# A two-layer hybrid decoder trunk: some accumulating DMAs become VectorE adds, and the FFN's four-pair groups, weight slots and raw tiles are dealt out anew

## The chip, the cores and the metric

The kernel runs on one core of a Trainium2 chip. The core's engines run side by side and wait for each other through semaphores: TensorE (PE, with the weight load PEld shown apart), VectorE (DVE), ScalarE (ACT), GpSimd (POOL) and SyncE (SP, which here only issues DMAs). The metric is device time in microseconds for one execution; lower is better.

## The reference

A residual stream of 256 tokens by 2048 goes through two layers, each a mixer and a SwiGLU FFN. All values are float32.

```python
def reference(x, ...):
    h = x
    for layer in range(DEPTH):              # DEPTH = 2
        xn = rms_norm(h, norm_mix[layer])
        if layer % 2 == 0:
            mix = swa_mlstm_mixer(xn, ...)  # sliding-window attention + mLSTM, out projection
        else:
            mix = forgetting_attention_mixer(xn, ...)
        h = h + mix
        h = h + swiglu(rms_norm(h, norm_ffn[layer]), w_gate[layer], w_up[layer], w_down[layer])
    return rms_norm(h, norm_final)

def swiglu(xn, w_gate, w_up, w_down):       # 2048 -> 5632 -> 2048
    return (jax.nn.silu(xn @ w_gate) * (xn @ w_up)) @ w_down
```

The change lies in the FFN.

## The kernel before, in words

**Products in split precision.** Each float32 matrix is used as a sum of two float32r parts, `hi` (a rounded copy, made by ScalarE) and `lo` (the rest, made by VectorE as `raw - hi`). A product is three matmuls: hi by hi, lo by hi, hi by lo (`three`, L531 to L534). The activations stand in `xh`, `xl` (and `mh`, `ml` for the FFN's hidden values), already split. The weights are streamed: `load_raw` (L134) issues a DMA from SP that brings 256 rows by 512 columns into a raw tile of 128 partitions by 2 by 512 (512 KB), `split_chunk` (L187, L188) or `split_plain` (L356, L357) splits it into a weight slot, a `hi` and a `lo` tile of the same size.

**Buffers.** In the FFN there are `RAWS` = 5 raw tiles. Weight slots are dealt out in a circle from `stock`: six of the pool `wp` and two (`more`) of the FFN's own pool, eight in all. A slot can be written again when TensorE has finished with it, and a raw tile can be loaded again when its readers have finished.

**Groups.** The hidden width 5632 is cut into 11 groups `g` of 512 columns. For a group, `pair_group` multiplies the activations (16 chunks of 128 rows, taken as 8 pairs) by `w_gate` and `w_up` at once. `PARTS` = (0, 3, 7, 11) cuts the groups into three parts: groups 0 to 2, 3 to 6, 7 to 10. Behind each part's groups stands its share of the down product, again by `pair_group`, over two column halves `n0`, and the result is added into `h`. In the last layer's last part the second half goes through `gemm` instead.

**Plain chunks and pairs.** An entry `(0, p)` of the order is plain: two chunks (gate and up) with 24 matmuls of 512 columns. An entry `(1, p)` is a *pair* in the sense used below: a scheme with seven products in place of eight, so 21 matmuls, for which sums of the weights and of the activations (`sums_of`) are needed. With `ra` the gate tile and `rb` the up tile, the weight side is:

```python
nc.gpsimd.dma_start(rb[:, 0, :], w[part, c0 : c0 + NB], accum_op=ALU.add)   # rb0 += ra0, from HBM
hg, lg = split_chunk(ra, NB)
split_plain(hu, lu, rb)
rb1 = rb0 - rb1             # L605, the third sum, written over rb
ra  = ra - rb1 (both halves)  # L607
split_plain(hc, lc, rb1); split_plain(hd, ld, ra)
```

The first sum is made by an *accumulating DMA* from GpSimd's queue (L599): it fetches the 256 KB of the gate weights a second time and adds them to what lies in `rb`. A pair takes four slots (`hg`, `hu`, `hc`, `hd`), a plain entry two. `ORDER` has three pairs in eight entries, `HEAVY` four; the groups in `DENSE` = (1, 4, 5, 8, 9) use `HEAVY`. `DOWN` gives the down product two pairs of six entries in the first part and three of eight in the others. So a layer has 38 pairs in the groups, and with 16 (layer 0) and 13 (layer 1) in the down products there are 105.

**Combining.** At a group's end ScalarE and VectorE join the products (`combine`, L555 to L559), add the plain sums (L671), apply SiLU (L673) and the product (L675); the hidden values are transposed by DMA and split into `mh`, `ml` by a `join` that is put off into the next group.

**What stands ahead of the FFN.** `out_proj` is the mixer's output projection; its results are added to `h` (L370), squared for the norm, turned by DMA transposes (L317), and split by `split_scaled` (L361, L362). Part of that is put off into the FFN's first group.

**Order.** The code is written in the order above; a scheduler then sets the order of each engine's instructions by its own estimates, so a change of one place can move instructions over a whole layer. Each engine runs its list strictly in order.

Of the kernel before, what the change touches and what calls it, by code (L numbers as in the profile page):

```python
# [17 lines left out]
P = 128  # L18
# [5 lines left out]
NB = 512  # L24
CK = 2
# [10 lines left out]
ORDER = ((0, 0), (1, 1), (0, 2), (1, 3), (0, 4), (1, 5), (0, 6), (0, 7))  # L36
HEAVY = ((1, 1), (0, 0), (1, 3), (0, 2), (1, 5), (0, 4), (1, 7), (0, 6))
FOURTH = 7
DENSE = (1, 4, 5, 8, 9)
DOWN = {  # L40
    6: ((0, 0), (1, 1), (0, 2), (1, 3), (0, 4), (0, 5)),
    8: ((0, 0), (1, 1), (0, 2), (1, 3), (0, 4), (1, 5), (0, 6), (0, 7)),
# [9 lines left out]
W_RAWS = 4  # L52
LATER = (6, 10, 3, 5)
LATER_DOWN = (5, 6)
RAWS = 5
P_JOIN = 4
COLD = 9
TURNED = (0,)
# [17 lines left out]
def trunk(  # L76
# [459 lines left out]
    def bank(par, name):  # L536
        return pm.tile([P, NB], F32, tag="pm", name=name) if par else pa.tile([P, NB], F32, tag="acc", name=name)

    def pair_group(fp, par, lhs, sums, mats, order, todo=(), halves=None, inner=None, raws=None):
        plain = [[bank(par, "acc") for _ in range(NT)] for _ in range(2)]  # L540
        begun = set()

        def fresh(*at):
            known = at in begun
            begun.add(at)
            return not known

        todo = list(todo)
        prods = None
        kinds = [kind for kind, _ in order]  # L550
        t0, t1 = slice(0, P), slice(P, 2 * P)

        def combine(prods):
            c = fp.tile([P, 4, NB], F32, tag="c", name="c", bufs=1)
            nc.scalar.copy(c[:, 0, :], prods[0])  # L555
            if halves is None:
                nc.vector.tensor_tensor(out=c[:, 1, :], in0=prods[3], in1=c[:, 0, :], op=ALU.add)
                nc.vector.tensor_tensor(out=c[:, 2, :], in0=prods[2], in1=c[:, 1, :], op=ALU.add)
                nc.vector.tensor_tensor(  # L559
                    out=c[:, 1:4:2, :],  # L560
                    in0=prods[1].rearrange("p (a n) -> p a n", a=1).broadcast_to([P, 2, NB]),
                    in1=c[:, 1:3, :],
                    op=ALU.subtract,
                )
                return c
            nc.vector.tensor_tensor(out=c[:, 2, :], in0=prods[3], in1=c[:, 0, :], op=ALU.add)
            nc.vector.tensor_tensor(out=c[:, 1, :], in0=prods[2], in1=c[:, 2, :], op=ALU.add)
            nc.vector.tensor_tensor(out=c[:, 3, :], in0=prods[1], in1=c[:, 1, :], op=ALU.subtract)
            nc.vector.tensor_tensor(out=c[:, 2, :], in0=prods[1], in1=c[:, 2, :], op=ALU.subtract)
            return c  # L570

        for pos, (kind, pair) in enumerate(order):
            k0 = 2 * pair
            if inner is not None and pos == len(order) - 1:
                c = combine(prods)
                inner()
            if not kind:
                last = pos == len(order) - 1
                walk = [(i, t) for i in range(CK) for t in range(NT)]
                if last:  # L580
                    walk.sort(key=lambda it: it[1])
                for m, (w, c0) in enumerate(mats):
                    hi, lo = load_chunk(w, k0, c0, NB)
                    run_due(todo, pos)
                    for i, t in walk:
                        ah, al = lhs(k0 + i)
                        ts = slice(t * P, (t + 1) * P)
                        three(
                            plain[m][t], ah[:, ts], al[:, ts], hi[:, i, :], lo[:, i, :],
                            fresh(m, t), last and i == CK - 1,  # L590
                        )
                continue
            first, last = 1 not in kinds[:pos], 1 not in kinds[pos + 1 :]
            if first:
                prods = [bank(1 - par, "prod") for _ in range(4)]
            ra, rb = (load_raw(w, k0, c0, NB, fp, W_RAWS if halves else RAWS, raws) for w, c0 in mats)
            if halves is None:
                (w, c0), part = mats[0], slice(k0 * P, (k0 + 1) * P)
                nc.gpsimd.dma_start(rb[:, 0, :], w[part, c0 : c0 + NB], accum_op=ALU.add)  # L599
            hg, lg = split_chunk(ra, NB)  # L600
            run_due(todo, pos)
            hu, lu = slot()
            if halves is None:
                split_plain(hu, lu, rb)
                nc.vector.tensor_tensor(out=rb[:, 1, :], in0=rb[:, 0, :], in1=rb[:, 1, :], op=ALU.subtract)  # L605
                both = rb[:, 1, :].rearrange("p (a n) -> p a n", a=1).broadcast_to([P, CK, NB])
                nc.vector.tensor_tensor(out=ra, in0=ra, in1=both, op=ALU.subtract)  # L607
                hc, lc = (a[:, 0, :] for a in slot())
                split_plain(hc, lc, rb[:, 1, :])
                hd, ld = slot()  # L610
                split_plain(hd, ld, ra)
                ht = [hu[:, 0, :], hd[:, 0, :], hc, hd[:, 1, :]]
                lt = [lu[:, 0, :], ld[:, 0, :], lc, ld[:, 1, :]]
            else:
                split_plain(hu[:, 1, :], lu[:, 1, :], rb[:, 1, :])
                nc.vector.tensor_tensor(out=ra[:, 0, :], in0=rb[:, 0, :], in1=ra[:, 0, :], op=ALU.add)
                nc.vector.tensor_tensor(out=rb[:, 0, :], in0=rb[:, 1, :], in1=rb[:, 0, :], op=ALU.subtract)
                nc.vector.tensor_tensor(out=rb[:, 1, :], in0=ra[:, 0, :], in1=rb[:, 1, :], op=ALU.subtract)
                nc.vector.tensor_tensor(out=ra[:, 1, :], in0=ra[:, 1, :], in1=rb[:, 1, :], op=ALU.subtract)
# [12 lines left out]
            three(prods[0], xa[:, t0], la[:, t0], hg[:, 0, :], lg[:, 0, :], first, last)  # L632
            three(plain[0][0], xb[:, t0], lb[:, t0], hg[:, 1, :], lg[:, 1, :], fresh(0, 0), False)
            three(plain[1][0], sh[3], sl[3], hu[:, 1, :], lu[:, 1, :], fresh(1, 0), False)
            three(prods[1], sh[0], sl[0], ht[0], lt[0], first, last)
            three(prods[2], sh[2], sl[2], ht[1], lt[1], first, last)
            three(prods[3], sh[1], sl[1], ht[2], lt[2], first, last)
            three(plain[0][1], xb[:, t1], lb[:, t1], ht[3], lt[3], fresh(0, 1), False)
        if inner is None:
            c = combine(prods)  # L640
        return plain, c

    def ffn(layer, fp, sx, x4, sd, key, todo, idx_next=None, key_next=None, finish=None):
# [8 lines left out]
        for g0, g1 in zip(PARTS, PARTS[1:]):  # L652
# [3 lines left out]
            for g in range(g0, g1):  # L656
# [6 lines left out]
                    [(w_gate[layer], g * NB), (w_up[layer], g * NB)],  # L663
                    HEAVY if g in DENSE else ORDER,
                    todo,
                )
                todo = []
                for m in range(2):
# [79 lines left out]
            for n0 in (0, 2):  # L748
                if end and idx_next is None and n0 == 2:
                    for n in (2, 3):  # L750
                        acc = new_acc()
                        gemm(acc, m_of, wd, n * NB, NB, 0, nk, nk, skew=3 if n == 3 else 1, halved=n == 3)
                        close(acc, n)
                    continue
                plain, c = pair_group(
                    fp, 1 - n0 // 2, m_of, sums_d, [(wd, n0 * NB), (wd, (n0 + 1) * NB)], order, todo
                )
                todo = []
                if end and idx_next is None:
                    gf = fp.tile([P, D], F32, tag="c", name="gf", bufs=1)  # L760
                    nc.gpsimd.dma_start(gf, norm_final.partition_broadcast(P))
                for t in range(NT):
                    o = h[:, t, n0 * NB : (n0 + 2) * NB]
                    nc.vector.tensor_tensor(
                        out=o, in0=c[:, 2 * t : 2 * t + 2, :].rearrange("p a n -> p (a n)"), in1=o, op=ALU.add
                    )
                for m in range(2):
                    close(plain[m], n0 + m)

    def close_layer(layer, w_out, idx, key, **rest):  # L770
        with tc.tile_pool(name=f"fp{layer}", bufs=2) as fp:
# [3 lines left out]
            x4 = fp.tile([P, 2, P], F32R, name="x4", bufs=1)  # L775
            todo = out_proj(w_out, idx, key, (*sx, x4, fp))
            sd = [fp.tile([P, nd, 4, P], F32R, tag=f"sd{i}", name=f"sd{i}", bufs=1) for i in range(2)]
            more = [[fp.tile([P, CK, NB], F32R, name=f"{a}{i}", bufs=1) for a in ("hi", "lo")] for i in range(2)]
            stock.extend(more + [slot() for _ in range(6)])
            ffn(layer, fp, sx, x4, sd, key, todo, **rest)  # L780
            stock.clear()
# [601 lines left out]
```

## Time and profile before

| | |
|---|---|
| median of three runs | 2097.1 us (2096.4 to 2097.92) |
| the profiled execution | 2095.33 us, of which 2093.6 us are its span |
| granted TensorE clock, mean | 0.998 |
| PE busy | 2072.1 us (99%) |
| DVE busy | 1794.4 us (86%) |
| ACT busy | 1384.1 us (66%) |
| accumulating DMAs (L599) | 76 of gate, 29 of down weights |
| HBM read | 436.21 MB |

Stretches are given as from:to in us from the start of the span. In a row of the profile, L599 is line 599 of the kernel's file, `out<-in` are the names of the tiles, `xN` the count of instructions, and `[5.27 <-DMA raw...]` the idle time of the engine just before and what ended it. Layer 0's FFN follows its `out_proj` near 330; its first part ends near 530, the second near 775 and the third near 1015. Layer 1's FFN begins near 1400, and its parts end near 1597, 1840 and 2045.

### The profile page before, as it was taken

The numbers are of one execution on the slowest core, as the hardware profiler recorded it, in microseconds if no ns is written. First come the engines' busy times: TensorE is split into PE (matmuls) and PEld (weight loads), VectorE is DVE, ScalarE is ACT, GpSimd is POOL, SyncE is SP. The second block draws the span as 40 slices with busy tenths as digits, with TensorE's granted clock in tenths as the row PEclk, the third lists the DMA queues.
The fourth block names the chain that finished last, engine by engine and source line by source line (L and its number), as shares of the span: only waits on it lengthen the run. The fifth ranks groups of instructions, "written<-read, shape, count | busy, mean of one in ns | idle before, by whom it ended". The sixth has DMA issues, their size and how long they took to land.

```text
span 2093.6 us, 27094 instructions
## 1 busy us (share of the span) xinstructions
PE 2072.1 (99%) x9443; PEld 1709.8 (82%) x9443; DVE 1794.4 (86%) x2217; ACT 1384.1 (66%) x1764; POOL 133.7 (6%) x171
## 2 busy tenths in 40 slices
PE   9999999999999999999999999999999999999998
PEld 8878887778888888888888888887788888888887
DVE  6788768988999998998899678578899999999995
ACT  6767677665567656667676776686655667557763
POOL 1010000000000000000000001000000000000000
PEclk9999999999999999999999999999999999999999
DMA  8666578777788777887676777597778777867864
GB/s 294 177 201 201 195 257 226 217 215 218 220 229 265 227 244 220 237 238 202 204 225 198 227 201 186 162 263 202 243 220 244 228 223 234 265 201 209 263 208 150
DMA packets 324698, 462.43 MB, mean 221 GB/s; under 512 B 108092, under 2 KB 116304, under 8 KB 324432
## 3 DMA queue, kind: packets, MB, share of 16 engines
q1 hardware_dynamic: 307088, 426.27, 64.8%
q0 software_dynamic: 16752, 33.33, 9.0%
q8 instruction: 74, 1.21, 0.2%
q10 hardware_dynamic: 720, 1.09, 0.1%
q14 instruction: 64, 0.52, 0.1%
HBM read 436.21 MB, written 2.12 MB: 209 GB/s over the span
## 4 chain that ended last, share of the span: by engine, by line
PE 75%; DVE 8%; DMA 6%; ACT 5%; issue 4%; SPq 0%; ACTq 0%; POOLq 0%; POOL 0%; DVEq 0%
PE acc L533 16%; PE acc L532 16%; PE acc L534 16%; PE prod L533 4%; PE prod L532 4%; PE prod L534 4%; PE acc L222 4%; PE acc L223 4%; PE acc L224 4%; DVE lo L188 2%; DVE lo L357 2%; DMA raw<-in_w_down_dram 2%; ACT hi L187 2%; DMA raw<-in_w_gate_dram 1%; ACT hi L356 1%
## 5 line engine op out<-in xcount | busy, mean ns | idle before, releaser
L188 DVE TENSOR_TENSOR lo<-raw,hi 128x1024 fp32r<-128x1024 f32 (+2 forms) x646 | 761.7, 1194 | 153.8 <-ACT hi L187 151.2
L187 ACT CAST hi<-raw 128x1024 fp32r<-128x1024 f32 (+2 forms) x646 | 651.6, 1026 | 319.8 <-PE acc L534 83.7
L533 PE MATMUL acc<-lo,xh 128*128 128x512 f32 x1260 | 491.7, 391 | 1.0 <-DVE lo L188 1.0
L534 PE MATMUL acc<-hi,xl 128*128 128x512 f32 x1260 | 490.1, 390 | 0.0
L532 PE MATMUL acc<-hi,xh 128*128 128x512 f32 x1260 | 478.6, 392 | 5.5 <-ACT hi L187 3.9
L356 ACT CAST hi<-raw 128x1024 fp32r<-128x1024 f32 (+1 forms) x329 | 291.4, 894 | 226.5 <-DVE raw L605 84.6
L357 DVE TENSOR_TENSOR lo<-raw,hi 128x1024 fp32r<-128x1024 f32 (+1 forms) x329 | 334.9, 1029 | 52.2 <-ACT hi L356 50.8
L532 PEld LDWEIGHTS acc<-hi,xh 128*128 128x128 f32 x1260 | 236.8, 188 | 58.8 <-ACT hi L187 7.7
L533 PEld LDWEIGHTS acc<-lo,xh 128*128 128x128 f32 x1260 | 236.8, 188 | 53.0 <-DVE lo L188 3.9
L534 PEld LDWEIGHTS acc<-hi,xl 128*128 128x128 f32 x1260 | 236.9, 188 | 48.9
L533 PE MATMUL acc<-lo,mh 128*128 128x512 f32 x466 | 181.6, 390 | 0.0
L534 PE MATMUL acc<-hi,ml 128*128 128x512 f32 x466 | 181.4, 389 | 0.0
L532 PE MATMUL acc<-hi,mh 128*128 128x512 f32 x466 | 175.8, 390 | 0.5 <-ACT hi L187 0.5
L607 DVE TENSOR_TENSOR raw<-raw 128x1024 f32<-128x1024 f32 x105 | 128.3, 1222 | 1.0
L599 POOL DMA_DIRECT2D raw<-in_w_gate_dram x76 | 65.1, 856 | 963.9 <-DMA raw<-in_w_up_dram 391.4
L223 PE MATMUL acc<-lo,mh 128*128 128x512 f32 (+1 forms) x322 | 126.3, 392 | 0.0
L222 PE MATMUL acc<-hi,mh 128*128 128x512 f32 (+1 forms) x322 | 125.8, 391 | 0.0
L224 PE MATMUL acc<-hi,ml 128*128 128x512 f32 (+1 forms) x322 | 123.7, 391 | 0.0
L532 PEld LDWEIGHTS acc<-hi,mh 128*128 128x128 f32 x466 | 87.5, 188 | 19.4 <-ACT hi L187 1.3
L533 PEld LDWEIGHTS acc<-lo,mh 128*128 128x128 f32 x466 | 87.5, 188 | 18.1
L534 PEld LDWEIGHTS acc<-hi,ml 128*128 128x128 f32 x466 | 87.5, 188 | 18.1
L223 PE MATMUL acc<-lo,xh 128*128 128x512 f32 (+3 forms) x288 | 99.7, 347 | 0.2 <-DVE lo L188 0.2
(361 smaller groups left out, 3093.3 us busy)
## 6 DMA issues: line engine op xcount, KB each, us to landing
raw<-in_w_gate_dram SPq DMA_DIRECT2D x176, 512.0 KB, 5.2
raw<-in_w_up_dram SPq DMA_DIRECT2D x176, 512.0 KB, 5.4
raw<-in_w_down_dram SPq DMA_DIRECT2D x176, 512.0 KB, 5.7
raw<-in_w_in_odd_dram SPq DMA_DIRECT2D x88, 512.0 KB, 5.3
raw<-in_w_in_even_dram SPq DMA_DIRECT2D x51, 512.0 KB, 4.8
raw<-in_w_gate_dram POOLq DMA_DIRECT2D x76, 256.0 KB, 5.7
raw<-in_w_out_even_dram SPq DMA_DIRECT2D x32, 512.0 KB, 5.4
raw<-in_w_out_odd_dram SPq DMA_DIRECT2D x32, 512.0 KB, 4.8
```

The source lines that it names most:

```text
L187: latest[0] = nc.scalar.copy(hi[:, k, 0:n], raw[:, k, 0:n])
L188: nc.vector.tensor_tensor(out=lo[:, k, 0:n], in0=raw[:, k, 0:n], in1=hi[:, k, 0:n].bitcast(F32), op=ALU.subtract)
L222: nc.tensor.matmul(o, ah[:, ts], hi, start=(k == 0), stop=False)
L223: nc.tensor.matmul(o, ah[:, ts], lo, start=False, stop=False)
L224: nc.tensor.matmul(o, al[:, ts], hi, start=False, stop=(k == k_all - 1 and cs.stop == n))
L356: nc.scalar.copy(dst_h, src)
L357: nc.vector.tensor_tensor(out=dst_l, in0=src, in1=dst_h.bitcast(F32), op=ALU.subtract)
L532: nc.tensor.matmul(o, ah, hi, start=start, stop=False)
L533: nc.tensor.matmul(o, ah, lo, start=False, stop=False)
L534: nc.tensor.matmul(o, al, hi, start=False, stop=stop)
L599: nc.gpsimd.dma_start(rb[:, 0, :], w[part, c0 : c0 + NB], accum_op=ALU.add)
L607: nc.vector.tensor_tensor(out=ra, in0=ra, in1=both, op=ALU.subtract)
```

## The change

Four things change together.

- The accumulating DMA is used only where `adding` is set, which is from the second part on (`g0 >= ADDING`, `ADDING` = 3). In the first part, groups and down product, VectorE adds `ra0` to `rb0` instead.
- The third sum goes to a tile of its own, `t3`, instead of over `rb`, and is made ahead of the split of `rb`.
- `DENSE` becomes (3, 4, 5, 7, 8, 9): group 1 has three pairs, groups 3 and 7 have four.
- There are seven weight slots instead of eight, and six raw tiles instead of five.

```diff
-DENSE = (1, 4, 5, 8, 9)
+DENSE = (3, 4, 5, 7, 8, 9)
+ADDING = 3
...
-RAWS = 5
+RAWS = 6
...
-            if halves is None:
+            if adding:
                 (w, c0), part = mats[0], slice(k0 * P, (k0 + 1) * P)
                 nc.gpsimd.dma_start(rb[:, 0, :], w[part, c0 : c0 + NB], accum_op=ALU.add)
             hg, lg = split_chunk(ra, NB)
             run_due(todo, pos)
             hu, lu = slot()
             if halves is None:
+                if not adding:
+                    nc.vector.tensor_tensor(out=rb[:, 0, :], in0=ra[:, 0, :], in1=rb[:, 0, :], op=ALU.add)
+                t3 = fp.tile([P, NB], F32, tag="t3", name="t3")
+                nc.vector.tensor_tensor(out=t3, in0=rb[:, 0, :], in1=rb[:, 1, :], op=ALU.subtract)
                 split_plain(hu, lu, rb)
-                nc.vector.tensor_tensor(out=rb[:, 1, :], in0=rb[:, 0, :], in1=rb[:, 1, :], op=ALU.subtract)
-                both = rb[:, 1, :].rearrange("p (a n) -> p a n", a=1).broadcast_to([P, CK, NB])
+                both = t3.rearrange("p (a n) -> p a n", a=1).broadcast_to([P, CK, NB])
                 nc.vector.tensor_tensor(out=ra, in0=ra, in1=both, op=ALU.subtract)
                 hc, lc = (a[:, 0, :] for a in slot())
-                split_plain(hc, lc, rb[:, 1, :])
+                split_plain(hc, lc, t3)
...
+                    adding=g0 >= ADDING,          # the groups' call of pair_group
...
-                    fp, 1 - n0 // 2, m_of, sums_d, [...], order, todo
+                    fp, 1 - n0 // 2, m_of, sums_d, [...], order, todo, adding=g0 >= ADDING
...
-            more = [[...] for i in range(2)]
+            more = [[...] for i in range(1)]
             stock.extend(more + [slot() for _ in range(6)])
```

A layer then has 39 pairs in the groups instead of 38, and there are 107 pairs in all, 81 of them with an accumulating DMA and 26 with an add. In the changed file the add is L606, the third sum L608 and the subtraction from `ra` L611; the accumulating DMA is L600, and other lines of the helpers above move by one. The change in the instructions' order is shown with the prediction, at GpSimd and at VectorE.

More of the change, by code (lines that the diff above doesn't have):

```diff
@@ L537, in bank, with pair_group @@
         return pm.tile([P, NB], F32, tag="pm", name=name) if par else pa.tile([P, NB], F32, tag="acc", name=name)
-    def pair_group(fp, par, lhs, sums, mats, order, todo=(), halves=None, inner=None, raws=None):
+    def pair_group(fp, par, lhs, sums, mats, order, todo=(), halves=None, inner=None, raws=None, adding=False):
         plain = [[bank(par, "acc") for _ in range(NT)] for _ in range(2)]
@@ L755, in ffn @@
                 plain, c = pair_group(
-                    fp, 1 - n0 // 2, m_of, sums_d, [(wd, n0 * NB), (wd, (n0 + 1) * NB)], order, todo
+                    fp, 1 - n0 // 2, m_of, sums_d, [(wd, n0 * NB), (wd, (n0 + 1) * NB)], order, todo, adding=g0 >= ADDING
                 )
@@ L777, in close_layer @@
             sd = [fp.tile([P, nd, 4, P], F32R, tag=f"sd{i}", name=f"sd{i}", bufs=1) for i in range(2)]
-            more = [[fp.tile([P, CK, NB], F32R, name=f"{a}{i}", bufs=1) for a in ("hi", "lo")] for i in range(2)]
+            more = [[fp.tile([P, CK, NB], F32R, name=f"{a}{i}", bufs=1) for a in ("hi", "lo")] for i in range(1)]
             stock.extend(more + [slot() for _ in range(6)])
```

## The prediction

> **What bounds the kernel now.** I read the engine totals first, then the stretches of the FFN one beside the other, then the waits inside the stretches that fall short, last the rows around those waits.
>
> ```profile
> PE 2072.1 (99%) x9443; PEld 1709.8 (82%) x9443; DVE 1794.4 (86%) x2217; ACT 1384.1 (66%) x1764; POOL 133.7 (6%) x171
> ```
>
> TensorE looks full everywhere, but matmuls are pipelined, so its busy time hides short stalls. The count of matmuls in a stretch does not. In the rows below (busy us of PE, weight load, DVE, ACT, POOL, each with its instructions, then granted clock, DMA share and GB/s) the two stretches of 100 us are the yardstick: 443 matmuls, one every 100/443 = 0.226 us.
>
> ```profile
> 318.00:340.00 22.00, 22.00 (x99) 18.22 (x98) 14.95 (x23) 19.02 (x29) 1.55 (x2) 1.00 0.85 205
> 340.00:360.00 20.00, 19.18 (x80) 14.31 (x80) 20.00 (x28) 17.32 (x25) 0.88 (x1) 1.00 0.74 223
> 360.00:380.00 20.00, 18.99 (x82) 14.91 (x81) 16.46 (x21) 7.75 (x10) 1.72 (x2) 1.00 0.68 185
> 380.00:420.00 40.00, 38.63 (x161) 31.02 (x160) 36.93 (x43) 30.06 (x33) 2.56 (x3) 0.96 0.84 244
> 420.00:460.00 40.00, 38.86 (x168) 30.94 (x167) 34.74 (x40) 26.90 (x30) 2.56 (x3) 1.00 0.72 216
> 460.00:530.00 70.00, 69.72 (x312) 57.41 (x311) 63.47 (x69) 34.72 (x39) 4.28 (x5) 1.00 0.71 212
> 600.00:700.00 100.00, 100.00 (x443) 82.82 (x442) 94.81 (x109) 68.28 (x76) 6.84 (x8) 1.00 0.82 235
> ...
> 1405.00:1425.00 20.00, 18.76 (x76) 13.62 (x75) 20.00 (x31) 18.71 (x26) 0.89 (x1) 1.00 0.63 188
> 1425.00:1440.00 15.00, 13.53 (x57) 10.43 (x56) 11.65 (x16) 7.85 (x9) 0.84 (x1) 1.00 0.62 194
> 1440.00:1480.00 40.00, 39.08 (x168) 30.83 (x167) 37.06 (x43) 26.98 (x31) 3.39 (x4) 1.00 0.92 254
> 1480.00:1530.00 50.00, 48.14 (x202) 38.42 (x201) 43.97 (x53) 31.89 (x36) 2.60 (x3) 0.97 0.70 209
> ...
> 1900.00:2000.00 100.00, 100.00 (x443) 82.80 (x442) 96.36 (x113) 70.10 (x78) 7.69 (x9) 1.00 0.81 241
> ```
>
> In layer 0's first part 340:460 should hold 4.43 matmuls per us and lacks 8.6, 6.6, 16.2 and 9.2 of them: 40.6 x 0.226 = 9.2 us. In layer 1's, 1405:1530 lacks 12.6, 9.4, 9.2 and 19.5: 50.7 x 0.226 = 11.4 us. So 20.6 us of TensorE time are lost in the first FFN parts (groups 0 to 2 and their down product), and nothing in 600:700 or 1900:2000. At the two entries, 340:360 and 1405:1425, VectorE is 20.00 of 20 us busy; after them it has gaps, so something else holds it. The rows of ScalarE, VectorE's source of `hi`, show what:
>
> ```profile
> 365.37 1.57 ACT L356 CAST hi<-raw 128x1024 fp32r<-128x1024 f32 x2 [5.27 <-DMA raw<-in_w_gate_dram]
> ...
> 380.63 1.04 ACT L356 CAST hi<-raw 128x1024 fp32r<-128x1024 f32 x1 [4.12 <-PE prod L534]
> ...
> 428.25 1.05 ACT L356 CAST hi<-raw 128x1024 fp32r<-128x1024 f32 x1 [5.84 <-DMA raw<-in_w_gate_dram]
> ...
> 1447.63 1.05 ACT L356 CAST hi<-raw 128x1024 fp32r<-128x1024 f32 x1 [3.31 <-DMA raw<-in_w_gate_dram]
> ```
>
> Three of the four waits, of some 3 to 6 us, are for the accumulating DMA. It can be issued only when the tile's own load has landed, and then takes as long again, which layer 1's chain shows as two transfers end to end ahead of the cast at 1447.63:
>
> ```profile
> 1437.85 3.78 DMA raw<-in_w_up_dram
> 1441.70 0.54 issue
> 1442.25 5.22 DMA raw<-in_w_gate_dram
> ```
>
> The fourth, at 380.63, is a wait for a weight slot that TensorE had not yet released.
>
> **The adds (26 of 105 pairs).** In the first parts, 3 x 3 pairs in the groups and 2 x 2 in the down product, twice over, lose the accumulating DMA and get an add on VectorE. GpSimd shows it:
>
> ```order
> L599 DMA raw<-in_w_gate_dram 128x512 x3
> L254 TENSOR_TENSOR r<-tot,mhalf 128x2
> L599 DMA raw<-in_w_gate_dram 128x512 x7
> L599 DMA raw<-in_w_down_dram 128x512 x4
> L599 DMA raw<-in_w_gate_dram 128x512 x14
> ```
>
> After the change (lines moved by one):
>
> ```order
> L1113 TENSOR_TENSOR st<-st,mhalf 128x2 x4
> L255 TENSOR_TENSOR r<-tot,mhalf 128x2
> L600 DMA raw<-in_w_gate_dram 128x512 x15
> L600 DMA raw<-in_w_down_dram 128x512 x6
> L600 DMA raw<-in_w_gate_dram 128x512 x15
> ```
>
> Ten gate and four down DMAs go in front of part 1; each later part has 15 gate DMAs instead of 14. `r` no longer stands behind three of them, which I price at nothing: by the code the SiLU, the first to read it, stands behind all the products of group 0 and their sums. The median time to landing of such a DMA, and rows from which an add's time can be read:
>
> ```profile
> raw<-in_w_gate_dram POOLq DMA_DIRECT2D x76, 256.0 KB, 5.7
> ```
> ```profile
> 564.62 0.69 DVE L605 TENSOR_TENSOR raw<-raw 128x512 f32<-128x512 f32 x1
> 565.22 0.75 DVE L675 SCALAR_TENSOR_TENSOR c<-c,r 128x512 f32<-128x512 f32 x1
> 565.88 1.22 DVE L607 TENSOR_TENSOR raw<-raw 128x1024 f32<-128x1024 f32 x1
> 567.01 0.69 DVE L357 TENSOR_TENSOR lo<-raw,hi 128x512 fp32r<-128x512 f32 x1
> ```
>
> The latency behind the load falls from 5.7 us to one 128x512 VectorE instruction. That one occupies VectorE from its start to the next one's: 565.22 - 564.62 = 0.60 us; a 128x1024 one 567.01 - 565.88 = 1.13 us. Thirteen adds a layer are 7.8 us more VectorE work.
>
> **Where they land.** On VectorE, out_proj's tail before, then after:
>
> ```order
> L357 TENSOR_TENSOR lo<-raw,hi 128x1024
> L188 TENSOR_TENSOR lo_3095<-raw,hi_3094 128x1024
> L605 TENSOR_TENSOR raw<-raw 128x512
> L188 TENSOR_TENSOR lo_3097<-raw,hi_3096 128x1024
> L370 TENSOR_TENSOR h<-acc,h 128x512
> ```
> ```order
> L606 TENSOR_TENSOR raw<-raw 128x512
> L363 SCALAR_TENSOR_TENSOR xl<-box,gT,xh 128x256 x3
> L275 TENSOR_TENSOR s_2956<-full 128x128
> L608 TENSOR_TENSOR t_3160<-raw 128x512
> L273 TENSOR_TENSOR s_2956<-full 128x128
> L606 TENSOR_TENSOR raw<-raw 128x512
> L274 TENSOR_TENSOR s_2956<-s_2956,full 128x128
> L608 TENSOR_TENSOR t_3249<-raw 128x512
> ```
>
> The first two pairs' add (L606) and third sum (L608) have moved well ahead of the residual adds, into a place where VectorE is idle 22.00 - 14.95 = 7 us (318:340). So at the entry, where VectorE is full, one add per layer is left: +0.6 x 2 = +1.2 us.
>
> **The four-pair groups.** A pair is 21 matmuls instead of 24. Group 1 loses its fourth pair, groups 3 and 7 get one: per layer 3 matmuls fewer, so 6 x 0.226 = -1.4 us. On VectorE a pair is four 128x1024 and two 128x512 instructions, 4 x 1.13 + 2 x 0.60 = 5.7 us, against 2 x 1.13 for the two plain chunks: 3.5 us leave the first part and enter each later one. A later part lasts some 245 us (530 to 775), so that is 1.4% more on VectorE's 94.81 in 600:700; I price it at nothing as long as the slack of `hi` and `lo` covers it, and otherwise it belongs to the slower rival below.
>
> **What the first parts give back.** Behind the entries, 360:460 and 1425:1530 lack 32.0 and 38.1 matmuls, 7.2 and 8.6 us. VectorE there does 88.1 of 100 and 92.7 of 105 us. With some 8 of the 13 adds falling in (4.8) and the fourth pair out (3.5), it has 89.4 and 94.0 us to do, in 100 - 7.2 + 0.7 = 93.5 and 105 - 8.6 + 0.7 = 97.1 us if TensorE were never stopped (0.7 for group 1's three extra matmuls): 96% and 97%. The 1900:2000 row is 96.36% with TensorE full, so this is just at the edge of what the kernel does elsewhere. Ends: nothing comes back, or 15.8 us. I take 9, a little over half, since the accumulate waits go wholly but the slot wait doesn't. Part of the loss is the clock:
>
> ```profile
> 384.41 0.63 PE L533 MATMUL prod<-lo,sx 128*128 128x512 f32 x1
> 384.83 0.63 PE L534 MATMUL prod<-hi,sx 128*128 128x512 f32 x1
> ```
> ```profile
> PE prod L532 <- ACT hi L356: 1.4, 2, 0.9
> ```
>
> These start 0.42 us apart, not 0.226, in the stretch whose granted clock is 0.96, and the second row (TensorE's waits in 318:530: us in total, times, longest) has TensorE's longest wait there, 0.9 us. That is counted in the missing matmuls. The Trainium skill (TensorE: Matmul & The Clock Gate, Part 1) has the clock halve only after an idle window of about 3.4 us; by that the stalls would cost their own length alone and return less. This trace disagrees: the half rate follows stalls far shorter than that.
>
> **Own tile, slots, raw tiles.** The third sum was written over `rb`, so it waited until `rb` had been split; ScalarE's cast then waited for the split's L605:
>
> ```profile
> ACT hi L356 <- DVE raw L605: 19.4, 8, 4.6
> ...
> ACT hi L187 <- PE prod L534: 14.4, 6, 4.6
> ```
> ```profile
> PE prod L533 <- DVE lo L357: 0.4, 1, 0.4
> ```
>
> The first two are waits of ScalarE in part 1 of layer 0 (530:775; us in total, times, longest), the third is the only wait of TensorE in 530:1000, where groups 4, 5, 8 and 9 already have four pairs. The first row shrinks; TensorE is full there, so it gives no time, only slack. The second is the price of slots with eight of them; a group with four pairs uses 4 x 4 + 4 x 2 = 24 slots in 180 x 0.226 = 40.7 us, 1.7 us a slot, so with one slot less a cast may start 1.7 us later. No trace shows seven slots: between 0 (slack covers it) and 1.7 us in each of 12 such groups, 20 us. I take +1, near the lower end, since TensorE waits only those 0.4 us. A sixth raw tile starts loads earlier; where TensorE is full it gives nothing.
>
> **Sum**, against the profiled execution (2095.33 us, 2093.6 of it span; 1.8 us under the median of 2097.1): -9 - 1.4 + 1.2 + 1 = -8.2, so 2087.1, and at the median 2088.9: I say **2089 us**.
>
> **Rivals.**
> *Seven slots starve the four-pair groups (slower).* Three now stand in a row (3, 4, 5 and 7, 8, 9). It decides once ScalarE's slack in them is under 1.7 us. For it: the 14.4 us of slot waits above, and TensorE's one wait for `lo`. Against: no matmul is missing in 600:700 and 1900:2000, both in later parts. All of it costs 20 us, and with the front's 9 + 1.4 - 1.2 = 9.2 returned the time is 2097.1 + 20 - 9.2 = 2108; from 13.4 us on it is over 2101.3, and four fifths of it, 16 us, give 2104. Chance 0.20. The Trainium skill (Perfetto Trace Analysis, Optimization Strategy) reads a gap that repeats on the engine that should be full as too few buffers; it speaks against a slot less, and no row yet shows such a gap in these groups.
> *VectorE takes over the front.* The accumulate wait becomes a queue of adds on an engine at 96 to 97%; only the six matmuls remain, less the entry's 1.2, so 2097, 2093 to 2101. For it: the two full entries. Chance 0.18.
> *All stalls go*, since they feed each other through the clock: -20.6 - 1.4, about 2075. The busy entries speak against. Chance 0.10.
>
> **Numbers.** Forecast 0.52, its own range 2082 to 2095. Outside 2078 to 2103 lie most of "all stalls go" and the worst third of the slower rival with its tail, near 0.2. A measurement tells some 0.2%, 4.2 us. Faster than 2092.9: all of 0.10 and nearly all of 0.52, 0.62 with a bit of the edge; same 0.18; slower 0.20.
>
> **What would show it.** Right: 340:460 and 1405:1530 hold more matmuls, the waits of L356 for gate DMAs are gone in the first parts, L606 appears 26 times, 600:700 keeps 443. Wrong: TensorE waits for `hi` or `lo` in groups 3 to 5 or 7 to 9, or VectorE stays at 20 of 20 us beyond the entry with the stalls as long as before.

## The result, and the profile after

The changed kernel takes 2132.1 us (median of four runs, 2125.8 to 2139.8), the kernel before in the same session 2096.8 (four runs): a ratio of 1.0169, 95% interval 1.015 to 1.0188. It is 35 us slower; 2089 was forecast, with 2078 to 2103 as the range. The profiled execution took 2134.66 us, 2132.9 of them span.

The engines' totals of the changed kernel hide it, as they did before: TensorE is 98% busy.

```profile
PE 2085.4 (98%) x9437; PEld 1713.4 (80%) x9437; DVE 1811.1 (85%) x2251; ACT 1389.1 (65%) x1768; POOL 116.8 (5%) x147
```

The matmuls in equal stretches show it. First the kernel before, then the changed one (columns as in the prediction):

```profile
340.00:460.00 120.00, 115.66 (x486) 91.19 (x486) 108.13 (x130) 82.04 (x97) 7.72 (x9) 0.99 0.75 221
530.00:780.00 250.00, 250.00 (x1105) 207.08 (x1104) 233.79 (x255) 160.97 (x177) 17.06 (x20) 1.00 0.80 237
1405.00:1530.00 125.00, 119.51 (x499) 93.30 (x498) 112.67 (x139) 85.43 (x100) 7.72 (x9) 0.99 0.75 218
1600.00:1850.00 250.00, 250.00 (x1105) 207.04 (x1104) 232.34 (x253) 161.39 (x176) 17.09 (x20) 1.00 0.78 234
```
```profile
340.00:460.00 120.00, 119.14 (x525) 98.08 (x524) 115.85 (x145) 81.91 (x95) 0.00 (x0) 1.00 0.70 215
530.00:780.00 250.00, 240.78 (x1037) 195.26 (x1036) 220.66 (x244) 153.00 (x167) 18.16 (x21) 0.99 0.78 226
...
1405.00:1530.00 125.00, 122.58 (x536) 99.83 (x535) 113.69 (x144) 92.61 (x114) 1.61 (x1) 1.00 0.72 212
1600.00:1850.00 250.00, 240.29 (x1039) 195.00 (x1038) 220.92 (x243) 155.90 (x171) 17.10 (x20) 0.99 0.77 219
1900.00:2000.00 100.00, 95.42 (x404) 77.01 (x403) 88.00 (x102) 63.59 (x71) 7.69 (x9) 0.97 0.77 221
```

The first parts hold 39 and 37 matmuls more, 76 x 0.226 = 17 us. But the later parts, where no matmul was missing, now lack 68 in 530:780, 66 in 1600:1850 and 39 of 443 in 1900:2000; the first two alone are 134 x 0.226 = 30 us. In layer 1 such a stretch does not hold quite the same work in both kernels, since the changed one comes there 21 us later. The last matmul of each part's down product (the last that reads `mh`, `ml` or `sd`) marks the same place of the work in both. It starts at (us):

| up to the end of | before | changed | behind by | of it in this part |
|---|---|---|---|---|
| layer 0, first part | 519.78 | 511.42 | -8.4 | -8.4 |
| layer 0, second part | 767.30 | 773.56 | 6.3 | +14.6 |
| layer 0, third part | 1016.52 | 1037.54 | 21.0 | +14.8 |
| layer 1, first part | 1588.13 | 1600.67 | 12.5 | -8.5 |
| layer 1, second part | 1835.65 | 1863.63 | 28.0 | +15.4 |
| the span | 2093.6 | 2132.9 | 39.3 | +11.3 |

So the first parts gave back 17 us, and the later ones took 56. VectorE is less busy in 530:780 than before, not more (220.66 against 233.79 us). What it waits for stands in its groups (busy, mean ns, then idle just before and what ended it):

```profile
L608 DVE TENSOR_TENSOR t<-raw 128x512 f32<-128x512 f32 x107 | 73.6, 688 | 91.4 <-DMA raw<-in_w_gate_dram 42.4 <-issue 28.5 <-DMA raw<-in_w_down_dram 17.9
```

L608 is the third sum in its own tile. Before, the same sum (L605) had 1.0 us of idle time ahead of it:

```profile
L605 DVE TENSOR_TENSOR raw<-raw 128x512 f32<-128x512 f32 x105 | 72.3, 689 | 1.0
```

And TensorE waits for `lo` (us in total, times, longest):

```profile
PE acc L534 <- DVE lo L189: 18.1, 13, 4.0
PE prod L534 <- DVE lo L358: 12.3, 10, 3.3
```

One such wait, in the down product of layer 0's second part, followed through the timeline (start, us, instruction, idle before it), first GpSimd, then VectorE, ScalarE and TensorE:

```profile
750.67 0.86 POOL L600 DMA_DIRECT2D raw<-in_w_gate_dram  x1 [12.99 <-DMA raw<-in_w_up_dram]
```
```profile
749.32 0.69 DVE L358 TENSOR_TENSOR lo<-t,hi 128x512 fp32r<-128x512 f32 x1
755.31 0.69 DVE L608 TENSOR_TENSOR t<-raw 128x512 f32<-128x512 f32 x1 [5.31 <-DMA raw<-in_w_gate_dram]
755.92 1.22 DVE L189 TENSOR_TENSOR lo<-raw,hi 128x1024 fp32r<-128x1024 f32 x1
757.05 1.22 DVE L358 TENSOR_TENSOR lo<-raw,hi 128x1024 fp32r<-128x1024 f32 x1
```
```profile
749.43 1.05 ACT L357 CAST hi<-raw 128x1024 fp32r<-128x1024 f32 x1 [1.47 <-DVE raw L611]
750.39 1.04 ACT L188 CAST hi<-raw 128x1024 fp32r<-128x1024 f32 x1
```
```profile
754.64 0.39 PE L533 MATMUL prod<-hi,sd 128*128 128x512 f32 x1
758.32 0.80 PE L534 MATMUL prod<-lo,sd 128*128 128x512 f32 x1 [3.29 <-DVE lo L358]
758.92 0.63 PE L535 MATMUL prod<-hi,sd 128*128 128x512 f32 x1
759.34 0.63 PE L533 MATMUL prod<-hi,sd 128*128 128x512 f32 x1
...
764.03 0.39 PE L535 MATMUL acc<-hi,ml 128*128 128x512 f32 x1
```

The accumulating DMA is issued at 750.67; it brings gate weights, so the pair is one of the next group. The sum that needs it stands next in VectorE's list and stops the engine from 750.00 to 755.31. Behind it stand `lo` tiles that do not need that DMA: ScalarE had the `hi` of 749.43 ready at 750.48, yet its `lo` (L358) is made at 757.05, and this is the one that TensorE waits for. TensorE stands still for 3.29 us and runs on at one matmul in 0.43 us until 764.03:

```profile
758.00:764.00 6.00, 5.68 (x13) 4.46 (x14) 6.00 (x8) 1.66 (x2) 0.33 (x1) 0.50 0.95 309
```

Thirteen matmuls in those 5.71 us instead of 25 are another 2.8 us. So this one early sum costs some 6 us of TensorE.

### The profile page after: what moved, and what is told of

Read it like the earlier page. It is cut to its first block, busy times and chain, and to the rows that moved or that the text cites. A ratio compares the mean times of both kernels' runs of the same rounds, so it can differ in the third digit from the quotient of the medians.

```text
span 2132.9 us, 26958 instructions
## 1 busy us (share of the span) xinstructions
PE 2085.4 (98%) x9437; PEld 1713.4 (80%) x9437; DVE 1811.1 (85%) x2251; ACT 1389.1 (65%) x1768; POOL 116.8 (5%) x147
## 4 chain that ended last, share of the span: by engine, by line
PE 49%; DVE 22%; DMA 16%; issue 9%; ACT 4%; SPq 0%; DVEq 0%; POOLq 0%; ACTq 0%; POOL 0%
PE acc L534 10%; PE acc L535 9%; PE acc L533 9%; DVE lo L189 8%; DMA raw<-in_w_gate_dram 6%; DVE lo L358 5%; DMA raw<-in_w_up_dram 5%; PE acc L224 4%; PE acc L223 4%; PE acc L225 4%; DMA raw<-in_w_down_dram 3%; PE prod L533 2%; DVE raw L611 2%; PE prod L534 2%; PE prod L535 2%
## 5 line engine op out<-in xcount | busy, mean ns | idle before, releaser
L534 PE MATMUL acc<-lo,xh 128*128 128x512 f32 x1248 | 490.8, 393 | 15.4 <-DVE lo L189 15.3
L533 PE MATMUL acc<-hi,xh 128*128 128x512 f32 x1248 | 466.2, 393 | 1.9 <-ACT hi L357 1.0
L357 ACT CAST hi<-raw 128x1024 fp32r<-128x1024 f32 (+1 forms) x228 | 232.5, 1024 | 143.4 <-DVE raw L611 87.5
L534 PEld LDWEIGHTS acc<-lo,xh 128*128 128x128 f32 x1248 | 236.1, 189 | 70.5 <-DVE lo L189 20.9
L358 DVE TENSOR_TENSOR lo<-raw,hi 128x1024 fp32r<-128x1024 f32 (+1 forms) x228 | 269.8, 1187 | 6.9 <-ACT hi L357 6.9
L608 DVE TENSOR_TENSOR t<-raw 128x512 f32<-128x512 f32 x107 | 73.6, 688 | 91.4 <-DMA raw<-in_w_gate_dram 42.4
L611 DVE TENSOR_TENSOR raw<-raw,t 128x1024 f32<-128x1024 f32 x107 | 130.6, 1220 | 0.5
L600 POOL DMA_DIRECT2D raw<-in_w_gate_dram x60 | 51.7, 861 | 931.9 <-DMA raw<-in_w_up_dram 212.8
```

The costliest lines, as they stand in the source:

```text
L357: nc.scalar.copy(dst_h, src)
L358: nc.vector.tensor_tensor(out=dst_l, in0=src, in1=dst_h.bitcast(F32), op=ALU.subtract)
L533: nc.tensor.matmul(o, ah, hi, start=start, stop=False)
L534: nc.tensor.matmul(o, ah, lo, start=False, stop=False)
L608: nc.vector.tensor_tensor(out=t3, in0=rb[:, 0, :], in1=rb[:, 1, :], op=ALU.subtract)
```

## The experiments

**Theory.** The own tile takes away the only thing that kept the third sum late: written over `rb`, it had to wait for `rb`'s split. Free of that, it is put early into VectorE's list, and where it needs an accumulating DMA it blocks the `lo` tiles behind it. **Rivals:** seven slots or the list `DENSE` starve the four-pair groups; the tile itself costs (its memory, or `rb` coming free earlier); VectorE has too much to do.

### The third sum

**Undone alone.** The changed kernel with

```diff
-                t3 = fp.tile([P, NB], F32, tag="t3", name="t3")
-                nc.vector.tensor_tensor(out=t3, in0=rb[:, 0, :], in1=rb[:, 1, :], op=ALU.subtract)
                 split_plain(hu, lu, rb)
+                t3 = rb[:, 1, :]
+                nc.vector.tensor_tensor(out=t3, in0=rb[:, 0, :], in1=rb[:, 1, :], op=ALU.subtract)
```

> The changed kernel with the third sum back over rb, behind rb's split; everything else of the change stays (adds in the first part, four pairs in groups 3, 4, 5, 7, 8, 9, seven slots, six raw tiles). Theory (VectorE stands at the third sum until the accumulating DMA has landed, 89 us of idle time ahead of L608, and the lo tiles behind it come late): the wait goes back to ScalarE, VectorE's idle time ahead of the third sum falls under 5 us, and the time to 2082 to 2095 us. Rival (seven slots starve the four-pair groups): little changes, 2115 to 2130. Rival (three four-pair groups in a row): 2115 to 2130 as well.

Measured: 2086.1 us (2083.6 to 2090.3), ratio to before 0.9961 [0.9947, 0.9974]. The own tile ahead of the split costs 46 us, more than the whole loss. The sum's group and the stretches:

```profile
L609 DVE TENSOR_TENSOR raw<-raw 128x512 f32<-128x512 f32 x107 | 73.6, 689 | 0.6
```
```profile
340.00:460.00 120.00, 116.27 (x510) 95.18 (x508) 111.40 (x139) 81.02 (x94) 0.00 (x0) 1.00 0.66 207
530.00:780.00 250.00, 249.72 (x1099) 205.69 (x1098) 234.39 (x256) 162.15 (x177) 18.14 (x21) 1.00 0.80 235
...
1405.00:1530.00 125.00, 122.35 (x528) 98.93 (x527) 117.11 (x144) 83.36 (x96) 0.00 (x0) 0.99 0.65 210
```

The idle time ahead of the sum is gone, and 530:780 holds 1099 matmuls instead of 1037.

**Done alone.** The kernel before with seven slots and six raw tiles, the own tile ahead of the split and nothing else of the change (`t3` as in the change's diff; that kernel without the tile is below, 2080.5 us).

> Seven slots and six raw tiles as in the run that gave 2080 us, accumulating DMAs everywhere and the old four-pair groups, with only the third sum moved to its own tile ahead of the split. Theory (VectorE stands at the third sum until the DMA has landed): VectorE idle ahead of that line by over 80 us, and 2120 to 2165 us. If the loss needs the new adds or the new four-pair groups beside it: under 2100.

Measured: 2168.8 us (2163.5 to 2174.1), ratio 1.0349 [1.0329, 1.037]: 88 us slower than the same without the tile, and 4 us above the range that was expected. More pairs have an accumulating DMA here (105 instead of 81), and VectorE stands longer ahead of the sum:

```profile
L605 DVE TENSOR_TENSOR t<-raw 128x512 f32<-128x512 f32 x105 | 72.1, 687 | 148.4 <-DMA raw<-in_w_gate_dram 80.5 <-DMA raw<-in_w_down_dram 41.0 <-issue 25.2
```

**Early sums without accumulating DMAs.** The changed kernel with `ADDING = 11`, so that VectorE adds in every part.

> The changed kernel with adds on VectorE in all parts, so no accumulating DMA at all; the third sum stays in its own tile ahead of the split. Theory: without the DMA nothing makes VectorE stand there, its idle time ahead of the third sum falls under 10 us, and although 81 adds, 49 us of VectorE work, come in, the time falls to 2085 to 2112 us. Rival (the own tile or its place ahead of the split costs by itself): 2125 or more. Rival (VectorE has no room for more): 2125 or more, with VectorE busy over 97% in the later parts.

Measured: 2111.5 us (2111.3 to 2115.8), ratio 1.0081 [1.0066, 1.0096]. The sums are as early as in the changed kernel, and wait for nothing; what VectorE waits for now is the tile's own load, ahead of the adds (L606):

```profile
L606 DVE TENSOR_TENSOR raw<-raw 128x512 f32<-128x512 f32 x107 | 73.3, 685 | 32.1 <-DMA raw<-in_w_up_dram 19.3 <-DMA raw<-in_w_down_dram 9.7 <-DMA raw<-in_w_gate_dram 2.9
L608 DVE TENSOR_TENSOR t<-raw 128x512 f32<-128x512 f32 x107 | 73.2, 684 | 0.3
```
```profile
530.00:780.00 250.00, 242.71 (x1041) 198.25 (x1040) 233.92 (x266) 153.63 (x168) 0.00 (x0) 0.98 0.65 204
```

That is 21 us better than the change, though VectorE has 81 adds more. So the wait that costs most is the one for the accumulating DMA, and it was worth more than all those adds. What makes up the 25 us that are left against in place (2086.1) is not shown: the adds are VectorE work, but in 530:780 it is busy for 233.92 of 250 us, no more than in place (234.39), and it stands still ahead of some of the adds. Adds everywhere with the sums in place were not run.

**Early only where VectorE adds.** The changed kernel with

```diff
+                if adding:
+                    split_plain(hu, lu, rb)
-                t3 = fp.tile([P, NB], F32, tag="t3", name="t3")
+                t3 = rb[:, 1, :] if adding else fp.tile([P, NB], F32, tag="t3", name="t3")
                 nc.vector.tensor_tensor(out=t3, in0=rb[:, 0, :], in1=rb[:, 1, :], op=ALU.subtract)
-                split_plain(hu, lu, rb)
+                if not adding:
+                    split_plain(hu, lu, rb)
```

> The changed kernel, but in the parts that use the accumulating DMA the third sum goes over rb's second slab behind the split of rb, as in the kernel before; in each layer's first part, where VectorE adds, it keeps its own tile ahead of the split. Theory (an early third sum harms only where it waits for an accumulating DMA): the sums in their own tile wait under 2 us in all, the later parts run as in the in-place kernel (1099 matmuls or more in 530:780), and the first parts as in the changed kernel (438 in 360:460): 2076 to 2089 us, equal to the in-place kernel's 2086.1 or up to 8 below it. Rival (the own tile costs by itself, by its memory or because the sum ahead of the split holds up the low half): in a first part that is full it loses what it did in the later parts, about 60 us over 107 pairs, or 0.5 us a pair for the 24 pairs of the first parts: 2092 to 2102.

Measured: 2081.7 us (2079.5 to 2082.0), ratio 0.9931 [0.9918, 0.9945]. As the theory has it; in the first part the own tile is even worth some 4 us against in place (2086.1). Neither kind of sum waits for a DMA:

```profile
L610 DVE TENSOR_TENSOR raw<-raw 128x512 f32<-128x512 f32 x81 | 55.4, 684 | 0.6
...
L610 DVE TENSOR_TENSOR t<-raw 128x512 f32<-128x512 f32 x26 | 17.7, 682 | 0.0
```

**Place or tile?** The changed kernel with the own tile, the sum bound behind the `lo` of `rb`'s split:

```diff
-                split_plain(hu, lu, rb)        # behind the sum
+                nc.scalar.copy(hu, rb)         # ahead of the sum
+                split_b = nc.vector.tensor_tensor(out=lu, in0=rb, in1=hu.bitcast(F32), op=ALU.subtract)
+                with tc.issue_after(split_b.ins):
+                    nc.vector.tensor_tensor(out=t3, ...)
```

> The changed kernel with the third sum still in its own tile, but bound to come behind the lo of rb's split on VectorE. Theory (it is the place in VectorE's list, not the tile): as with the sum in place, 2082 to 2095 us. If the tile itself (its buffers, what it does to the raw tiles' release) were to blame: 2120 or more.

Measured: 2105.0 us (2101.6 to 2108.1), ratio 1.0056 [1.0039, 1.0072]: neither. 27 of the 46 us go with the place, 19 stay. Two more runs followed. The first only writes the sum behind `split_plain`, unbound:

> The changed kernel with the own tile kept and the sum only written behind the split of rb in the program's text, with nothing that binds it there. The list still puts sums ahead of the lows that are ready: at the 41st sum two lows of split weights stand between the sum of one pair and work that needs it. Theory (place in the list ahead of a landed load is what costs): VectorE idles again ahead of its sums on DMAs, some 60 to 100 us in all, and the time is 2112 to 2135, near the changed kernel's 2132. Rival (the text's place decides, since the split then has the first claim): idle ahead of the sums under 10 us and 2086 to 2105.

Measured: 2136.2 us (2132.6 to 2136.6), ratio 1.0187 [1.0172, 1.0202]: as slow as the change (1 us above what was expected). Not the place in the code but the freedom of the list decides:

```profile
L609 DVE TENSOR_TENSOR t<-raw 128x512 f32<-128x512 f32 x107 | 73.8, 689 | 95.6 <-DMA raw<-in_w_gate_dram 42.6 <-issue 31.9 <-DMA raw<-in_w_down_dram 19.3
```

The second is the bound one with `bufs=1` for `t3`:

> The own tile bound behind rb's split (2105.0 with two tiles for the third sums) with one tile for them instead of two, so that the sum of a pair waits until the split and the difference of the pair before have read theirs. Of the 19 us by which the bound own tile was slower than in place (2086.1), theory A: sums of two pairs stand one behind the other in VectorE's list and hold up what ScalarE copies from them (its copies of t waited 102.5 us for the sums, of the in-place sums 52.1): one tile sets them apart, 2086 to 2098. Theory B: the early release of rb by the own tile moves loads and the rest of the list: no better, 2100 to 2110. Theory C: one tile is a new wait: 2112 to 2125.

Measured: 2096.3 us (2092.2 to 2099.6, ten runs), ratio 1.0001 [0.9991, 1.0011]. Nine of the 19 us go, which theory A allowed; but its wait, ScalarE for the sums, is only a little shorter. With two tiles, then with one:

```profile
ACT hi L357 <- DVE t L611: 102.5, 50, 5.4
```
```profile
ACT hi L357 <- DVE t L611: 86.7, 38, 4.6
```

In the one with one tile the second part is full again:

```profile
530.00:780.00 250.00, 250.00 (x1104) 206.81 (x1103) 235.64 (x258) 162.33 (x178) 18.19 (x21) 1.00 0.82 237
```

By the ends of the down products, as in the table above, its profiled execution is 1.1 and 6.4 us longer than the one in place in the two first parts and 3.3 us in layer 0's third, of 9.1 us in all. So most of what is left is lost in the first parts. There no accumulating DMA is used, and binding the sum is what differs from the run above that gained by its freedom. Why bound is worse than in place is not settled.

### The other parts of the change

**Slots and raw tiles.** The kernel before with seven slots and six raw tiles, then with seven slots and the old five:

```diff
-            more = [[...] for i in range(2)]
+            more = [[...] for i in range(1)]
-RAWS = 5
+RAWS = 6        # not in the second
```

> The kernel before with seven weight slots and six raw tiles and nothing else of the change. Theory: TensorE stays ahead nowhere worse than a few us, 2094 to 2105. Rival (seven slots starve the groups): 2110 to 2130.

> The kernel before with seven weight slots and still five raw tiles. Seven slots with six raw tiles gave 2080 us, 15 less than before. If the sixth raw tile made that gain (loads, and with them the accumulating DMAs, are issued earlier): 2095 to 2110 here, the first parts' waits for the accumulating DMA back. If the seventh-for-eighth slot made it through another order of instructions: 2078 to 2086.

Measured: 2080.5 us (2079.7 to 2081.2), ratio 0.9934 [0.9919, 0.9948], and 2105.1 us (2103.3 to 2106.4), ratio 1.0044 [1.0027, 1.006]. The slot costs 9 us, the raw tile gives 25. The first time lies below everything that was expected, so the gain of the sixth tile was not foreseen here either. With six raw tiles the first parts are nearly full though all their sums still come by accumulating DMA:

```profile
340.00:460.00 120.00, 119.07 (x524) 97.55 (x523) 113.82 (x137) 84.39 (x98) 8.57 (x10) 1.00 0.79 236
...
1405.00:1530.00 125.00, 124.16 (x549) 101.92 (x549) 118.98 (x142) 85.98 (x102) 8.53 (x10) 1.00 0.77 228
```

The reason stands in ScalarE's waits of the kernel before in 330:530, of which the six-tile run has none:

```profile
ACT hi L356 <- DMA raw<-in_w_gate_dram: 11.1, 2, 5.8
```

The loads, and with them the accumulating DMAs, come earlier: the tenth accumulating DMA of the FFN is issued at 404.5 us with six tiles and at 425.1 with five and the same slots. With five tiles and seven slots ScalarE has such waits again (5.7 us in 330:530), and TensorE waits for `hi` (the whole run):

```profile
PE prod L532 <- ACT hi L356: 10.5, 6, 4.0
```

**A seventh raw tile**, in the run with six (2080.5) and in the in-place one (2086.1):

> The kernel before with seven weight slots and seven raw tiles (the run with six gave 2080.5, with five 2105.1). Theory (raw tiles let loads start earlier; the sixth removed nearly all waits, since with six TensorE waited under 3 us for a high or low half): the seventh finds little left, 2072 to 2082. Rival (loads stay the limit): another 10 us or more, below 2071. Memory could also be laid out worse: above 2084.

> The changed kernel with the third sum over rb's second slab behind its split (2086.1) and seven raw tiles in place of six. With adding DMAs a raw tile is held for two loads one after the other and is free later, so a further tile should give more here than in the kernel without VectorE's adds: 2072 to 2083 if the tiles still limit, 2084 to 2088 if VectorE's work in the first part is what is left.

Measured: 2084.9 us (ratio 0.9955 [0.9942, 0.9967]) and 2086.9 us (0.9963 [0.9951, 0.9976]): nothing more to gain. The first is 4 us slower than with six tiles, just inside the range that was named for a worse layout of memory; what makes the difference is not shown.

**The adds**, in the run with six raw tiles, in place, the list `DENSE` as before:

> Seven slots and six raw tiles, the third sum in place, the old four-pair groups, and the adds in the first part as the only other edit; with the run in place (2086, new four-pair groups) and the run of slots alone (2080) it tells what the adds and the groups are worth each. If the accumulating DMA still held the first part with six raw tiles: 2072 to 2079. If the sixth raw tile has already taken that away and the adds only load VectorE: 2080 to 2092.

Measured: 2099.6 us (2096.0 to 2101.3, ten runs), ratio 1.0014 [1.0005, 1.0024]. No expectation held: the adds cost 19 us here. With them 1405:1530 holds 491 matmuls instead of 549. They too stand in VectorE's list ahead of data that has not landed; how much of the 19 us comes from these waits, and how much from the work of the adds, was not separated:

```profile
L606 DVE TENSOR_TENSOR raw<-raw 128x512 f32<-128x512 f32 x28 | 19.2, 686 | 20.9 <-DMA raw<-in_w_up_dram 17.5 <-DMA raw<-in_w_down_dram 3.4
```
```profile
1405.00:1530.00 125.00, 115.27 (x491) 90.99 (x491) 114.47 (x144) 81.59 (x96) 0.00 (x0) 1.00 0.62 198
```

**The list `DENSE`**, first the old one in the changed kernel, then the new one in the run with six raw tiles (no adds, sums in place):

> The changed kernel with the old choice of four-pair groups (1, 4, 5, 8, 9). Theory: the waits at the third sum stay, 2118 to 2140 us. Rival (three four-pair groups in a row are too much for VectorE): most of the loss goes, 2095 to 2105.

> The kernel before with seven slots and six raw tiles (2080.5) and the changed kernel's four-pair groups 3, 4, 5, 7, 8, 9, accumulating DMAs everywhere, third sum in place. The list takes group 1's VectorE work out of the first part and six matmuls (1.4 us) out of the kernel, and brings work for two more groups to the later parts: theory 2076 to 2084 (the list gave 13.5 us only where VectorE had the first part's adds as well). Rival (the list is good by itself): 2063 to 2073. If the denser later groups run out of loads: 2086 to 2095.

Measured: 2162.0 us (ratio 1.0322 [1.0306, 1.0337]), above what was expected, with 126.8 us of idle time ahead of the early sums; and 2077.6 us (2076.9 to 2077.9), ratio 0.9915 [0.9901, 0.9928]. The new list is the better one beside the early sums (2132.1 against 2162.0), beside adds and sums in place (2086.1 against 2099.6) and, by 3 us, here. The second run is the fastest kernel of all, though its interval overlaps that of the same with the old list. Its first parts are the fullest, without a single add:

```profile
340.00:460.00 120.00, 119.94 (x533) 98.72 (x532) 112.88 (x135) 84.27 (x99) 8.58 (x10) 1.00 0.78 237
...
1405.00:1530.00 125.00, 124.88 (x555) 102.82 (x554) 117.12 (x138) 85.38 (x98) 7.69 (x9) 1.00 0.79 233
```

Laid end to end, part by part:

| one part more | us | step |
|---|---|---|
| before | 2096.8 | |
| seven slots | 2105.1 | +8 |
| six raw tiles | 2080.5 | -25 |
| the new `DENSE` | 2077.6 | -3 |
| adds in the first part, sums in place | 2086.1 | +9 |
| own tile ahead of the split (the change) | 2132.1 | +46 |

The runs stem from several sessions, in which the kernel before had medians of 2095.3 to 2096.8, so steps under 2 us mean little.

## Why the prediction was wrong

**The step that failed** is "Own tile, slots, raw tiles". I read the wait for `rb`'s split as slack to be had, and priced the own tile at nothing; it cost 46 us. The wait I wanted shorter was also what kept the sum from standing in VectorE's list ahead of a load that had not landed. The prediction's own row of VectorE's list showed L608 "moved well ahead", and I followed that only in the first part, where the operand comes from VectorE itself. In the later parts, what the sum needs comes by DMA, 5.7 us at the median in the prediction's row, and I did not ask what stands behind the sum while it waits. The Trainium skill (PSUM — Partial Sum Buffer, Engine vs sequencer instructions) says that VectorE's queue is strictly first in, first out; the trace agrees, with 4.8 us (750.48 to 755.31) in which a finished `hi` lay ready and VectorE stood idle at a sum that did not concern it. Of the 46 us the place in the list explains 27 to 31 (2105.0 with the sum bound, against 2132.1 and 2136.2); the rest hangs on the tile or on the binding, and its cause stays open.

**The first parts** returned 17 us instead of 9, so the direction was right and the size too small. (What could come back was a little more than the prediction's 20.6 us: its short stretches count a matmul on a border twice; in one piece, by 1105 in 250 us, 340:460 and 1405:1530 lack 44 and 54 matmuls, 22 us.) That the forecast came near here is luck, since the reason was wrong: beside six raw tiles the adds do not give this, they cost 9 us with the new list and 19 with the old, sums in place. The accumulate waits vanish with the sixth raw tile, which lets the tile's own load, and so the accumulating DMA behind it, start earlier. Whether the adds alone would have taken them away with five tiles, no run tells. I had priced that tile at nothing "where TensorE is full", and had not asked what it does where TensorE is not; it is the largest gain of the change, 25 us.

**The adds at the entry**, +1.2 us, were under-sized. By the ends of the down products, layer 0's first part is done after 511.7 us with the new list and no adds (2077.6), after 517.8 with adds and sums in place (2086.1) and after 511.4 in the changed kernel, with early sums; from layer 0's third part to the end of layer 1's first it takes 560.0, 565.6 and 563.1 us. So the adds cost 12 us in place and 3 us with early sums.

**The four-pair groups**, -1.4 us: measured -3 where nothing else is short, within what the intervals allow; where VectorE has the adds as well, 2099.6 against 2086.1, -13.5, and beside the early sums -30. The likely reason, not shown, is that group 1's lighter work lies where the adds fall.

**Seven slots**, +1 us, with 20 as the other end: measured +8 to 9 with five raw tiles. With six its price can't be read alone, since eight slots beside six tiles were not tried. The rival "seven slots starve the four-pair groups" had the right sign and not the cause: with the sums in place and the same seven slots and groups 530:780 holds 1099 matmuls, 1105 before.

**VectorE takes over** did not come true in the changed kernel, whose first parts gained. It is nearest in the run with adds, sums in place and the old list (2099.6), where the adds took back most of what the raw tile gave; there too VectorE stood idle for 20.9 us ahead of the adds, so a full queue is not what the trace shows. The sign I had named for being wrong, TensorE waiting for `lo` in groups 3 to 5 and 7 to 9, is what the trace shows (stalls of 1.2 to 1.5 us in groups 3 to 5, one of 3.3 in groups 7 to 9, for `lo`), by another cause than the rival's.

## What to carry to other kernels

Before a buffer is split to take away a dependency, ask what that dependency kept in order: on an engine that runs its list strictly in order, an instruction set free may be placed ahead of data that comes late, and then everything behind it waits too. So follow a moved instruction through every stage of the program, and look at where its operands come from in each. And when loads are chained (a load, then a DMA that adds onto it), the buffer that lets the first one start earlier can be worth more than replacing the second one.

## What the runs showed of the hardware

**The clock.** A stall of TensorE can cost more than its length. After the stall of 3.29 us above, matmuls came at 0.43 us for 5.7 us; after another of 3.29 us, before 1849.42, for 3.4 us. After single stalls of 1.19 and 1.38 us in the same trace they came at the full rate, after one of 2.07 us at half of it:

```profile
573.41 0.50 PE L534 MATMUL acc<-lo,xh 128*128 128x512 f32 x1 [1.38 <-DVE lo L189]
573.76 0.40 PE L535 MATMUL acc<-hi,xl 128*128 128x512 f32 x1
574.00 0.40 PE L534 MATMUL acc<-lo,xh 128*128 128x512 f32 x1
```
```profile
982.08 0.50 PE L534 MATMUL acc<-lo,mh 128*128 128x512 f32 x1 [2.07 <-DVE lo L189]
982.42 0.58 PE L535 MATMUL acc<-hi,ml 128*128 128x512 f32 x1
982.80 0.63 PE L534 MATMUL acc<-lo,mh 128*128 128x512 f32 x1
983.23 0.63 PE L535 MATMUL acc<-hi,ml 128*128 128x512 f32 x1
```

The rule of the Trainium skill that the prediction cited (TensorE: Matmul & The Clock Gate, Part 1: half rate after an idle window of about 3.4 us) does not fit these as the least length of a stall, since 2.07 us was enough. Nor does the length alone decide: in the run with the adds and the old list (2099.6), a stall of 2.65 us, before 1470.26, was followed by the full rate. The half rate that the prediction showed near 384 in the kernel before followed stalls of 0.9 us and less; there they stood close together:

```profile
381.73 0.50 PE L532 MATMUL prod<-hi,sx 128*128 128x512 f32 x1 [0.92 <-ACT hi L356]
...
383.62 0.56 PE L532 MATMUL prod<-hi,sx 128*128 128x512 f32 x1 [0.45 <-ACT hi L356]
383.98 0.63 PE L532 MATMUL acc<-hi,xh 128*128 128x512 f32 x1
```

So several short stalls within 3 us did here what a single one of 1.4 us did not. But three stalls of 0.58, 0.44 and 0.45 us between 1437 and 1440 in the same kernel were followed by the full rate. What is counted, these runs don't tell. The whole is not small: the granted clock of the span fell from 0.998 to 0.992, which is 0.002 x 2093.6 = 4 us before and 0.008 x 2132.9 = 17 us after, so by this estimate up to 13 of the 39 us are the slower clock that followed the stalls.
